# Expert layer of a two-block transformer: gate and up products with resting weights, free slots with an index past the last row

## Chip, cores and metric

One core of one Trainium2 chip runs one program. The metric is the device time of that program in microseconds (us), as a median over runs. TensorE (PE) has two clock levels, 1.2 and 2.4 GHz; the profile gives the granted clock as a share of the higher one.

## What is computed

512 tokens of 1024 features go through two transformer blocks. The first (latent attention, retention, convolution) and all of the second block but its last layer are not touched by the change. That last layer is a mixture of 16 experts; each token goes to 2 of them, both from one group of 4. `hf` below is the normalised token matrix (512 x 1024), `combine` holds for each token the weights of its two experts and zeros elsewhere, and the result is added to the residual.

```python
def _hier_moe(h, w_r1, b_r1, w_r2, b_r2, w_gate, w_up, w_down):
    ...
    g_sel = jnp.argmax(g_logits, axis=-1)
    ...
    top_p, top_i = lax.top_k(e_prob, EXPERT_TOPK)
    ...
    combine = jnp.sum(jax.nn.one_hot(expert_id, N_EXPERTS, dtype=jnp.float32)
                      * (g_w * top_p)[..., None], axis=1)
    hid = jax.nn.silu(jnp.einsum('nd,edf->nef', hf, w_gate)) * jnp.einsum('nd,edf->nef', hf, w_up)
    hid = hid * combine[..., None].astype(hid.dtype)
    out = jnp.einsum('nef,efd->nd', hid, w_down)
    return out.reshape(B, T, D)
```

Everything is float32. D_MODEL is 1024 and a hidden row of an expert has 256 features, so an expert has a gate and an up matrix of 1024 x 256 each and a down matrix of 256 x 1024.

## The kernel before

**Products of float32.** PE takes a fast form of float32 (float32r) that keeps fewer bits. A matrix that needs full accuracy is split into a high and a low float32r part (`split_w`, L337 on ACT rounds to the high part `wh`, L338 on DVE subtracts to the low part `wl`; both have a ring of three buffers), and `mm3` (L343 to L345) sums three products: high x high, low x high, high x low. A plain float32 matmul needs no split, and PE runs it as two passes, each with its own load of weights. "Weights" of a matmul, here, is the operand that rests in the PE array; the other moves through it.

**Experts.** An expert works on a block of NS = 96 slots. The experts' matrices come as 48 tiles of 1 MB (per expert: two tiles of gate and up side by side, four 128-row chunks of 512 columns each, then one of down), loaded by SP (`eraw`, `wraw` L1559) into NB = 14 buffers: N1 = 6, N0 = 2 and N2 = 3 buffers of their own and 3 of the general ring. A load past those waits for the load two before it; the thirteenth waits for the first gather.

**Routing** (`route`). For each of the four tiles of 128 tokens the block's last projection adds to the residual; `half` writes x times the norm's gain to a DRAM table `xgd` (Pool multiply L1608, store L1609) and x to the output (L1610), and forms the router's logits on PE (L1618). The norm's scale (`rsqrt`, L303 to L321) comes later and is not in `xgd`: it goes as two numbers per slot (`val`, L1713 to L1720) through a one-hot matmul (`look`, L1695) into `wsl`, and is applied in the tanh (L1790) and on the output (L1817, L1818). `slots` gives each slot the row it reads (L1745) and the row it adds to (L1748), which for a free slot is one of 96 spare rows behind the 512 of the output; these are written with x1 ahead of time (L1001).

**The loop.** For expert n: `gather` fetches 96 rows of `xgd` by an indirect DMA of Pool (L1763), PE transposes them (L1770, 8 times), ACT and DVE split them (L1772, L1773). `up`: the tokens rest (128 x 96) and the weights move (512 columns): 8 chunks x 3 matmuls into one PSUM bank of 96 x 512; then tanh L1790, L1791, L1792, two transposes back (L1795) and the split of the hidden rows (L1797 to L1800). For expert 0, Pool does the low part of three of the four splits (`n0`). `down`: hidden rows rest, two halves of 128 features; the second half is a plain float32 matmul (L1811) without a split, the first a split with 6 matmuls. Rows are weighted (L1817 on ACT, L1818 on DVE) and added to the output by an indirect DMA of Pool (L1819). In the program's loop, expert n's gather comes ahead of expert n-1's `up` and expert n-2's `down`; a scheduler sets the order on each engine. PSUM has four banks that `mm` hands out in turns.

Of the kernel before, what the change touches and what calls it, by code (L numbers as in the profile page):

```python
# [8 lines left out]
F32 = mybir.dt.float32  # L9
F32R = mybir.dt.float32r  # L10
# [10 lines left out]
RSK = 0.47077597149489786            # RSK * (t * t + RSB * t + RSC): t ** -0.5 within 3e-5 where RSQ brings t  # L21
# [103 lines left out]
class Cols:  # L125
    """Columns of a packed [128, n] array by name."""
# [18 lines left out]
def gain_cols(g):  # L145
    """Per-partition columns of the small vectors."""
# [25 lines left out]
def consts_a():  # L172
    """Tables of the first block: latent attention, retention."""
# [40 lines left out]
def consts_c():  # L214
# [10 lines left out]
    c.add("tok", np.stack([j, 512 + j], axis=1))  # L225
# [32 lines left out]
KT = [(48 + 128 * j, 128) for j in range(4)] + [(0, 48)]      # tiles of the compressed keys: tokens, the meta ones three times  # L258
# [4 lines left out]
class Kern:  # L263
# [14 lines left out]
    # ---- small helpers  # L278
# [18 lines left out]
    def rsqrt(s, ss, mult, name="rs", bufs=4):  # L297
        """(ss * mult + EPS) ** -0.5"""
# [16 lines left out]
        # y: the root with its sign turned; then a step of the third order and one of the second, both but for a factor  # L315
# [16 lines left out]
    def split_w(s, src, shape, eng=None):  # L332
        """src: [128, *shape] of 1024 elements -> (high, low) float32r parts"""
# [13 lines left out]
    def proj_f(s, raw, f, act, outs):  # L347
        """out[f-columns, tokens] for one 128-column half of a feature tile; outs: (psum, first token, tokens)"""
# [8 lines left out]
    def proj_all(s, raw, f, t0=0):  # L357
        """feature tile for the tokens from t0 on, the meta ones included: [(psum, their slice)]"""
# [9 lines left out]
    def proj_t(s, names, act, outs, by_tile=()):  # L368
        """out[tokens, 512 columns]; outs: (psum, first token, tokens); token tile by token tile in the halves by_tile"""
# [19 lines left out]
    def sumsq(s, src, n=128):  # L389
        """sums of squares of the rows of src"""  # L390
# [6 lines left out]
    def parts(s, p, sq):  # L397
        """sq in three exact bf16 parts; sq is spent"""
# [7 lines left out]
    def colsums(s, q, ps):  # L406
        """ps[token, tile]: sums over the rows of parts q"""
# [4 lines left out]
    def norm_T(s, src, n, gain, dst, off, ss=None):  # L412
        """rms-norm of n token rows, transposed into dst (high, low) at column off"""
# [17 lines left out]
    def split_y(s, y, k, scale=None):  # L431
        """y fp32 [128, 512] -> chunk k of yT"""
# [8 lines left out]
    # ---- block 1  # L441
# [56 lines left out]
    def silu2(s, p, z, tag, shape=None, bufs=2):  # L498
        """2 * silu(z)"""
# [8 lines left out]
    def rope_t(s, p, src, n, i, dst):  # L508
        """dst [n, 4, 64] = rope(src) by the token tables of tile i"""
# [58 lines left out]
            # states before each token tile, two heads on a diagonal  # L568
# [90 lines left out]
            # rotated shared keys, token-major  # L659
# [45 lines left out]
    def mla(s, lat, fill):  # L705
        nc, gc, id_ = s.nc, s.gc, s.id
        with s.pool("ml", 2) as p:
# [24 lines left out]
            def pull(n):  # L732
                """n more projections of convolution and gates"""
# [5 lines left out]
            def prep(g):  # L739
                """keys, values and queries of two heads"""  # L740
# [70 lines left out]
            def front(g):  # L811
                """scores and their exponentials, by query tiles"""
# [698 lines left out]
class Kern3(Kern2):  # L1511
    def moe(s):
        nc, a = s.nc, s.a
        with ExitStack() as c3:
# [12 lines left out]
            for n in range(N1 + N0, N1 + N0 + NF):  # L1527
                s.eraw(n)
# [373 lines left out]
```

## Time and profile before

| quantity | value |
|---|---|
| runs | 1320.57, 1323.01, 1323.64 us |
| median | 1323.01 us |
| span of the profiled execution, first to last instruction | 1319.7 us |
| PE busy | 1253.8 us, 95% of the span |
| DVE, ACT, POOL busy | 815.0, 585.1, 157.1 us |
| expert stage, first transposes to last matmul | 1136.8 to 1307.0 us |
| DMA share in most of that stage (1141 to 1240 us) | 1.01 |

The records do not say which of the three runs was profiled; the median is 3.3 us above the span. In the profile, a line such as L1763 is a line of the kernel, "out<-in" are the program's names of tiles, PEld is the load of weights, and a DMA share of 1.00 means that all 16 DMA engines of the core are busy throughout.

### The profile page before, as it was taken

What the parts mean: (1) busy time and instruction counts of PE and PEld (TensorE: products, weight loads), DVE (VectorE), ACT (ScalarE), POOL (GpSimd) and SP (SyncE); (2) the same over time, 40 slices, a digit from 0 to 9 for tenths busy, and PEclk for the clock granted to TensorE, in tenths of its full rate; (3) what the DMA queues carried; (4) which work ended last, traced back from release to release, by engine and by line L of the source; (5) the groups of instructions that cost most, each with busy time, mean ns of one, the idle gap of its engine ahead of it and who ended that gap; (6) DMA issues with size and microseconds to landing.
All of it is one profiled execution on the core that took longest, in us unless ns stands there. A gap on an engine that the chain in (4) does not pass through costs nothing. (4 is left out here: it accounts for less than half of the span.)

```text
span 1319.7 us, 17112 instructions
## 1 busy us (share of the span) xinstructions
PE 1253.8 (95%) x6356; PEld 982.0 (74%) x6356; DVE 815.0 (62%) x1869; ACT 585.1 (44%) x1053; POOL 157.1 (12%) x194
## 2 busy tenths in 40 slices
PE   6999999999999999999989999999999998799985
PEld 4788777877886787887777887888888887566652
DVE  6356776656866899325677534465563245898863
ACT  4233455444564453223556326333332243377762
POOL 0330110100000000000211111000002213223211
PEclk9999999999999999999999999999999999799997
DMA  7212121034541102222110131321245365699994
GB/s 260 98 65 80 49 73 41 25 106 170 210 159 66 52 34 76 96 96 72 58 64 33 65 125 36 116 76 61 100 150 192 109 236 182 195 320 314 313 287 120
DMA packets 31566, 164.12 MB, mean 124 GB/s; under 512 B 3746, under 2 KB 6690, under 8 KB 15588
## 3 DMA queue, kind: packets, MB, share of 16 engines
q1 hardware_dynamic: 27028, 147.65, 32.2%
q0 software_dynamic: 3584, 12.58, 4.4%
q10 hardware_dynamic: 864, 2.72, 0.6%
q8 instruction: 52, 0.85, 0.3%
q14 instruction: 38, 0.31, 0.1%
HBM read 150.36 MB, written 12.98 MB: 124 GB/s over the span
## 5 line engine op out<-in xcount | busy, mean ns | idle before, releaser
L338 DVE TENSOR_TENSOR wl<-raw,wh 128x1024 fp32r<-128x1024 f32 x167 | 213.5, 1279 | 177.2 <-ACT wh L337 166.5
L337 ACT ACTIVATE wh<-raw 128x1024 fp32r<-128x1024 f32 x167 | 176.4, 1059 | 312.5 <-PE mmp L344 216.5
L344 PE MATMUL mmp<-hl,wh 128*128 128x512 f32 (+1 forms) x488 | 192.6, 395 | 0.0
L343 PE MATMUL mmp<-hh,wh 128*128 128x512 f32 (+1 forms) x488 | 192.5, 395 | 0.0
L345 PE MATMUL mmp<-hh,wl 128*128 128x512 f32 (+1 forms) x488 | 192.1, 394 | 0.3 <-DVE wl L338 0.3
L345 PEld LDWEIGHTS mmp<-hh,wl 128*128 128x128 f32 x488 | 91.9, 188 | 19.7 <-issue 1.0
L343 PEld LDWEIGHTS mmp<-hh,wh 128*128 128x128 f32 x488 | 91.8, 188 | 19.3 <-issue 1.0
L344 PEld LDWEIGHTS mmp<-hl,wh 128*128 128x128 f32 x488 | 91.8, 188 | 18.6 <-issue 0.8
L338 DVE TENSOR_TENSOR wl<-eraw,wh 128x1024 fp32r<-128x1024 f32 x62 | 75.6, 1222 | 17.7 <-ACT wh L337 15.8
L337 ACT ACTIVATE wh<-eraw 128x1024 fp32r<-128x1024 f32 x65 | 68.7, 1057 | 25.7 <-PE mmp L345 15.4
L344 PE MATMUL mmp<-yl,wh 128*128 128x512 f32 x192 | 75.8, 396 | 0.0
L345 PE MATMUL mmp<-yh,wl 128*128 128x512 f32 x192 | 75.7, 395 | 0.0
L343 PE MATMUL mmp<-yh,wh 128*128 128x512 f32 x192 | 75.5, 396 | 0.0
L343 PE MATMUL mmp<-uh,wh 128*128 128x512 f32 (+3 forms) x160 | 55.6, 347 | 1.1 <-DVE cz L493 1.1
L344 PE MATMUL mmp<-ul,wh 128*128 128x512 f32 (+3 forms) x160 | 56.0, 351 | 0.0
L345 PE MATMUL mmp<-uh,wl 128*128 128x512 f32 (+3 forms) x160 | 55.2, 345 | 0.0
L343 PE MATMUL mmp<-wh,xh 128*96 128x512 f32 x128 | 52.3, 409 | 0.0
L343 PE MATMUL mmp<-wh,yh 128*128 128x512 f32 x128 | 50.6, 401 | 1.6 <-DVE xr L929 1.4
L345 PE MATMUL mmp<-wh,yl 128*128 128x512 f32 x128 | 51.9, 408 | 0.0
L344 PE MATMUL mmp<-wl,yh 128*128 128x512 f32 x128 | 51.7, 404 | 0.0
L344 PE MATMUL mmp<-wl,xh 128*96 128x512 f32 x128 | 51.4, 402 | 0.0
L345 PE MATMUL mmp<-wh,xl 128*96 128x512 f32 x128 | 50.6, 395 | 0.0
(546 smaller groups left out, 2751.4 us busy)
## 6 DMA issues: line engine op xcount, KB each, us to landing
raw<-in_wt_dram SPq DMA_DIRECT2D x85, 1024.0 KB, 5.0
eraw<-in_wt_dram SPq DMA_DIRECT2D x39, 1024.0 KB, 8.2
xin<-in_x_dram SPq DMA_DIRECT2D x4, 512.0 KB, 8.0
xr<-in_x_dram SPq DMA_DIRECT2D x4, 512.0 KB, 4.3
x<-xr SPq DMA_DIRECT2D x4, 512.0 KB, 4.5
rxr<-x SPq DMA_DIRECT2D x8, 256.0 KB, 3.1
out_dram<-rxr SPq DMA_DIRECT2D x8, 256.0 KB, 2.1
xgd<-rxg SPq DMA_DIRECT2D x8, 256.0 KB, 3.0
```

What stands on the lines that cost most here:

```text
L337: nc.scalar.activation(h, src, AF.Copy)
L338: (eng or nc.vector).tensor_tensor(l, src, h.bitcast(F32), op=ALU.subtract)
L343: mm(ps, ah, bh, start=start, stop=False)
L344: mm(ps, ah, bl, start=False, stop=False)
L345: mm(ps, al, bh, start=False, stop=stop)
```

## The change

1. **`up` with resting weights.** A 128 x 128 piece of the weights rests and the tokens move. The first tile of an expert is taken as it is: 16 plain float32 matmuls (4 chunks x 4 column groups) with 96 moving columns. The second is split as before: 16 pairs of a matmul of `wh` with the tokens' high and low parts side by side (192 columns) and one of `wl` with the high part (96). So two of the four splits of `up` go, and half of the tokens' features needs no split. The result is the hidden rows transposed, in two PSUM banks (gate, up); a copy and an add join the two parts of each (L1799, L1800), and the two transposes of the hidden rows go.
2. **`down` splits both halves** of its tile: one split more, and 12 float32r matmuls in place of 6 and 2 plain ones. `ye` has 2 buffers instead of 3.
3. **Normalised table.** ACT multiplies x times gain by the norm's scale before the store to `xgd` (two instructions per token tile, and the stores come that much later); `wsl` is one number per slot, `V` has 6 columns instead of 9.
4. **Free slots** get an index of 512 or more, and gather and scatter skip what is past row 511. The spare rows' x1 store and `dst` go. As a skipped row leaves its buffer as it was, `blank` clears the four `xg` buffers once, on Pool.
5. **N2 is 4**, so NB is 15. Pool splits nothing for expert 0.

```diff
@@ constants, route
-N1, N0, N2 = (6, 2, 3)
+N1, N0, N2 = (6, 2, 4)
...
-                    nc.sync.dma_start(a['out'][T:], s.x1[:NS])
...
-            xg = q.tile([128, 512], F32, tag='xg', name='rxg', bufs=3)
+            xg = q.tile([128, 512], F32, tag='xg', name='rxg', bufs=5)
...
-            ts(hr[:, i:i + 1], r, 0.5, None, op0=ALU.mult)
+            for z in range(2):
+                xg = xgs.pop((i, z))
+                nc.scalar.activation(xg, xg, AF.Copy, scale=r)
+                nc.sync.dma_start(s.xgd[128 * i:128 * i + 128, 512 * z:512 * z + 512], xg)
@@ slots
-        nc.vector.tensor_copy(a, tb[:, :, 0])
-        tt(idx, tb[:, :, 1], a, op=ALU.add)
-        nc.vector.tensor_scalar(u, tb[:, :, 2], -1.0, 1.0, op0=ALU.mult, op1=ALU.add)
-        tt(a, tb[:, :, 1], a, op=ALU.add)
-        nc.vector.scalar_tensor_tensor(dst, u, s.ce['tok'][:NS, 1:2], a, op0=ALU.mult, op1=ALU.add)
+        nc.vector.tensor_scalar(a, tb[:, :, 2], -float(T), float(T), op0=ALU.mult, op1=ALU.add)
+        tt(a, a, tb[:, :, 0], op=ALU.add)
+        tt(idx, a, tb[:, :, 1], op=ALU.add)
@@ blank, gather
+        for _ in range(2):
+            s.nc.gpsimd.memset(p.tile([128, D], F32, tag='xg', name='xg', bufs=2)[:NS], 0.0)
...
+                                         bounds_check=T - 1, oob_is_err=False)
...
+            if z:
+                nc.scalar.activation(xs[:, :, 0], b, AF.Copy)
+                nc.vector.tensor_tensor(xs[:, :, 1], b, xs[:, :, 0].bitcast(F32), op=ALU.subtract)
+            else:
+                nc.scalar.activation(xf, b, AF.Copy)
@@ up
+        ps = [s.mm()[:, :4 * NS].rearrange('p (f z c) -> p f z c', f=2, z=2) for _ in range(2)]
+        w = raws[0].rearrange('p (k c) -> p k c', k=4)
+        for k in range(4):
+            for f in range(4):
+                mm(ps[f // 2][:, f % 2, 0], w[:, k, 128 * f:128 * f + 128], xf[:, k], start=k + f % 2 == 0, stop=False, skip_group_check=True)
+        w = raws[1].rearrange('p (k c) -> p k c', k=4)
+        for j in range(2):
+            h, l = s.split_w(w[:, 2 * j:2 * j + 2], [2, 512])
+            for kk in range(2):
+                k = 2 * j + kk
+                for f in range(4):
+                    fc = slice(128 * f, 128 * f + 128)
+                    mm(ps[f // 2][:, f % 2], h[:, kk, fc], xs[:, k], start=False, stop=False, skip_group_check=True)
+                    mm(ps[f // 2][:, f % 2, 0], l[:, kk, fc], xs[:, k, 0], start=False, stop=k == 3, skip_group_check=True)
+        for z in range(2):
+            nc.scalar.activation(gu[z], ps[z][:, :, 1], AF.Copy)
+            nc.vector.tensor_tensor(gu[z], gu[z], ps[z][:, :, 0], op=ALU.add)
+        nc.scalar.activation(th, gu[0], AF.Tanh, scale=0.5)
...
@@ down
-        for c in range(2):
-            nc.tensor.matmul(po[c], hf, w[:, 1, 512 * c:512 * c + 512], start=True, stop=False)
-        h, l = s.split_w(w[:, 0], [1024])
+        for k in range(2):
+            h, l = s.split_w(w[:, k], [1024])
...
-        y = p.tile([128, D], F32, tag='ye', name='ye', bufs=3)[:NS]
+        y = p.tile([128, D], F32, tag='ye', name='ye', bufs=2)[:NS]
```

On PE, one expert in the middle of the loop before (mmp is a PSUM bank of `mm`, atp one for transposes, xh and xl the tokens' parts, hs the hidden rows' parts, eraw and raw tiles of weights; eight times the three rows with xh and xl, two of which are left out here):

```order
L1770 MATMUL atp<-id,xg 128x96 x8
L343 MATMUL mmp<-wh,xh 96x512
L344 MATMUL mmp<-wl,xh 96x512
L345 MATMUL mmp<-wh,xl 96x512
...
L1811 MATMUL mmp<-eraw,hf 96x512 x2
L343 MATMUL mmp<-wh,hs 96x512
L1795 MATMUL atp<-id,eth 128x96 x2
```

After L1795 there follow five more of the rows with hs. And one expert after the change:

```order
L1769 MATMUL atp<-id,xg 128x96 x8
L1787 MATMUL mmp<-xf,eraw 128x96 x16
L1795 MATMUL mmp<-xs,wh 128x192
L1796 MATMUL mmp<-xs,wl 128x96
...
L343 MATMUL mmp<-wh,hs 96x512
L344 MATMUL mmp<-wl,hs 96x512
L345 MATMUL mmp<-wh,hs 96x512
```

The pair L1795, L1796 stands 16 times, the three rows with hs 4 times. 24 moving passes of 512 columns became 64 loads of 128 columns with 96 or 192 moving ones, and nothing of the next expert stands between two `down` matmuls.

On DVE, one expert in the middle after the change, where the first row is the low part of `down`'s second piece and the two rows L1800 release the two PSUM banks of `up`:

```order
L338 TENSOR_TENSOR wl<-eraw,wh 128x1024
L1800 TENSOR_TENSOR gu<-gu,mmp 128x192
L1803 SCALAR_TENSOR_TENSOR eth<-eth,gu 128x192
L338 TENSOR_TENSOR wl<-raw,wh 128x1024
L1800 TENSOR_TENSOR gu<-gu,mmp 128x192
L338 TENSOR_TENSOR wl<-raw,wh 128x1024
L1804 TENSOR_TENSOR eth<-eth,gu 128x192
L1823 TENSOR_SCALAR ye<-mmp,wsl 96x512
L1807 TENSOR_TENSOR hs<-eth,hs 128x192
```

The release of the second bank stands behind a split of the next expert's weights; ACT has the same pattern (wh, gu, eth, wh, gu, wh). Four splits per expert stand where there were five.

On Pool, ahead of the first gather, before:

```order
L1608 TENSOR_TENSOR rxg<-rxr,gff 128x512 x4
L338 TENSOR_TENSOR wl<-eraw,wh 128x1024
L1608 TENSOR_TENSOR rxg<-rxr,gff 128x512 x3
L338 TENSOR_TENSOR wl<-eraw,wh 128x1024 x2
L1608 TENSOR_TENSOR rxg<-rxr,gff 128x512
L1763 DMA xg<-xgd,idx 96x1024 x8
```

and now:

```order
L1754 MEMSET xg 96x1024 x2
L1608 TENSOR_TENSOR rxg<-rxr,gff 128x512 x8
L1754 MEMSET xg 96x1024 x2
L1761 DMA xg<-xgd,idx 96x1024 x8
```

The three splits went to DVE, and two memsets stand right ahead of the first gather; the second of them waits for the last stores of rxg to `xgd`, whose memory it takes over.

## Rows read from the trace of the kernel before

**Rows 1.** The page: busy time (share of the span) and instructions by engine.
```profile
PE 1253.8 (95%) x6356; PEld 982.0 (74%) x6356; DVE 815.0 (62%) x1869; ACT 585.1 (44%) x1053; POOL 157.1 (12%) x194
```
**Rows 2.** Windows: stretch, us, busy (instructions) by engine, PEclk, DMA share, GB/s.
```profile
1141.40:1240.00 98.60, 98.60 (x456) 64.48 (x454) 87.93 (x114) 76.88 (x113) 26.09 (x20) 1.00 1.01 312
1240.00:1297.00 57.00, 49.82 (x210) 32.02 (x209) 40.37 (x51) 33.73 (x51) 7.91 (x5) 0.94 0.91 292
```
**Rows 3.** DMA queues in 1136.8 to 1297 us: packets, MB, share of 16 engines.
```profile
q1 hardware_dynamic: 5184, 37.75, 66.8%
q0 software_dynamic: 3102, 10.87, 30.3%
```
**Rows 4.** Timeline of PE over one expert: start, duration, line, operation, tiles.
```profile
1174.92 0.82 PE L1770 MATMUL atp<-id,xg 96*128 96x96 f32 x8
...
1176.28 0.40 PE L343 MATMUL mmp<-wh,xh 128*96 128x512 f32 x1
...
1180.90 0.39 PE L345 MATMUL mmp<-wh,xl 128*96 128x512 f32 x1
...
1184.49 0.83 PE L1770 MATMUL atp<-id,xg 96*128 96x96 f32 x8
1185.10 0.45 PE L343 MATMUL mmp<-wh,xh 128*96 128x512 f32 x1
```
**Rows 5.** Timeline of PE, three places with short matmuls.
```profile
1106.31 0.99 PE L1618 MATMUL mmp<-wr,h2T 128*128 128x24 f32 x8
1107.14 0.47 PE L345 MATMUL mmp<-wh,yl 128*128 128x512 f32 x1
...
623.98 0.27 PE L343 MATMUL atp<-dkh,dq 128*128 128x128 f32 x1
...
624.20 0.40 PE L343 MATMUL atp<-dkh,dq 128*128 128x384 f32 x1
...
155.64 0.28 PE L345 MATMUL mmp<-uh,wl 128*128 128x258 f32 x1
...
157.07 0.28 PE L345 MATMUL mmp<-uh,wl 128*128 128x258 f32 x1
```
**Rows 6.** PEld by line: count, duration ns min/median/max, first and last start, forms.
```profile
L1770 PEld LDWEIGHTS atp<-id,xg x128: 137/141/231, 1136.8 to 1277.7; 96*128 96x128 f32 x128
L1618 PEld LDWEIGHTS mmp<-wr,h2T x64: 186/192/333, 1078.2 to 1125.5; 128*128 128x128 f32 x64
```
**Rows 7.** Groups by form, 1140 to 1300 us: busy, mean ns, idle before, releasers.
```profile
L338 DVE TENSOR_TENSOR wl<-eraw,wh 128x1024 fp32r<-128x1024 f32 x62 | 75.6, 1222 | 17.7 <-ACT wh L337 15.8
L337 ACT ACTIVATE wh<-eraw 128x1024 fp32r<-128x1024 f32 x62 | 65.5, 1057 | 21.1 <-PE mmp L345 10.8 <-DMA eraw<-in_wt_dram 7.4 <-SPq L1542 2.3
L1792 DVE TENSOR_TENSOR eth<-eth,mmp 96x256 f32<-96x256 f32 x16 | 6.7, 417 | 0.6
```
**Rows 8.** Timelines of DVE, POOL and PE at the start; last a group of POOL.
```profile
1121.44 2.26 DVE L321 SCALAR_TENSOR_TENSOR rs<-rsu,rsy 128x1 f32<-128x1 f32 x1
...
1126.48 0.16 DVE L321 SCALAR_TENSOR_TENSOR rs<-rsu,rsy 128x1 f32<-128x1 f32 x1
...
1121.34 2.35 POOL L338 TENSOR_TENSOR wl<-eraw,wh 128x1024 fp32r<-128x1024 f32 x1 [3.80 <-ACT wh L337]
...
1132.26 1.12 POOL L1763 DMA_INDIRECT xg<-xgd,idx  x1 [7.36 <-DVE val L1715]
...
1136.79 1.54 PE L1770 MATMUL atp<-id,xg 96*128 96x96 f32 x8 [1.00 <-DMA xg<-xgd,idx]
...
L1082 POOL MEMSET wa2f<- 96x512 f32 x1 | 0.5, 523 | 94.5 <-DMA raw<-in_wt_dram 94.5
```
**Rows 9.** The tail: last matmul of PE, a piece of the chain, last scatter.
```profile
1306.62 0.40 PE L345 MATMUL mmp<-wh,hs 128*96 128x512 f32 x1
...
1303.37 5.37 DMA out_dram<-ye,dst
...
1309.59 1.41 POOL L1819 DMA_INDIRECT out_dram<-ye,dst  x1 [4.81 <-DMA out_dram<-ye,dst]
```

More of the change, by code (lines that the diff above doesn't have):

```diff
@@ L224, in consts_c @@
     c.add("iota", np.tile(j[:NS], (128, 1)))
-    c.add("tok", np.stack([j, 512 + j], axis=1))
+    c.add("tok", j)
     c.add("nblk", np.tile(np.arange(NX), (128, 1)))
@@ L1598, in route @@
         oh = one("oh", 4, 2, NS, dt=BF)
-        r4, hr = one("r4", 4), one("hr", 4)
+        r4 = one("r4", 4)
         s.wk = q
@@ L1605, in half @@
             ss = s.sumsq(xv)
[L1606 removed]
+            xg = q.tile([128, 512], F32, tag="xg", name="rxg", bufs=5)
             rc = (slice(128 * i, 128 * i + 128), slice(512 * c, 512 * c + 512))
             nc.gpsimd.tensor_tensor(xg, xv, g[:, rc[1]], op=ALU.mult)
[L1609 removed]
+            xgs[i, c] = xg
             nc.sync.dma_start(s.a["out"][rc], xv)
@@ L1624, in get @@
             return xr
-        part = {}
+        part, xgs = {}, {}
         def done(i, c, xv, b):
@@ L1687, in route @@
         s.out_t("wp", get, done)
-        s.idx, s.dst, s.wsl = one("idx", 16, dt=I32), one("dst", 16, dt=I32), one("wsl", 16, 2)
-        tb = one("tb", 16, 6)
+        s.idx, s.wsl = one("idx", 16, dt=I32), one("wsl", 16)
+        tb = one("tb", 16, 3)
         def look(z0, z1):
@@ L1696, in look @@
             return pi
-        s.slots(look(0, 3), 16, s.idx, s.dst)
+        s.slots(look(0, 3), 16, s.idx)
         ge, sg, w, sw = one("ge", 4, 4), one("sg", 4), one("w", 4, 2), one("sw", 4)
@@ L1709, in route @@
         tt(w, w, sw[:, :, None].to_broadcast([128, 4, 2]), op=ALU.mult)
[L1711 to L1722 removed]
+        ts(w, w, 0.5, None, op0=ALU.mult)
+        for z in range(3):
+            cp(V[:, :, :, 3 + z], w)
+            if z < 2:
+                tt(w, w, V[:, :, :, 3 + z], op=ALU.subtract)
+        fill(0, 4, 3, 6)
+        cp(tb[:NS], look(3, 6))
         s.weights(tb, s.wsl)
@@ L1753, in weights, with blank @@
         tb, wsl = tb[:NS], wsl[:NS]
-        t3 = tb.rearrange("p e (v z) -> p e v z", z=3)
-        tt(wsl, t3[:, :, :, 0], t3[:, :, :, 1], op=ALU.add)
-        tt(wsl, wsl, t3[:, :, :, 2], op=ALU.add)
+        tt(wsl, tb[:, :, 0], tb[:, :, 1], op=ALU.add)
+        tt(wsl, wsl, tb[:, :, 2], op=ALU.add)
+    def blank(s, p):
+        for _ in range(2):
+            s.nc.gpsimd.memset(p.tile([128, D], F32, tag="xg", name="xg", bufs=2)[:NS], 0.0)
     def gather(s, idx, p=None):
@@ L1816, in down @@
-        y = p.tile([128, D], F32, tag="ye", name="ye", bufs=3)[:NS]
-        nc.scalar.activation(y[:, :512], po[0], AF.Copy, scale=wsl[:NS, 1:2])
-        nc.vector.tensor_scalar(y[:, 512:], po[1], wsl[:NS, 1:2], None, op0=ALU.mult)
+        for k in range(2):
+            h, l = s.split_w(w[:, k], [1024])
+            for c in range(2):
+                cs = slice(512 * c, 512 * c + 512)
+                s.mm3(po[c], hh[:, k], hl[:, k], h[:, cs], l[:, cs], k == 0, k == 1)
+        y = p.tile([128, D], F32, tag="ye", name="ye", bufs=2)[:NS]
@@ L1819, in down @@
+        nc.scalar.activation(y[:, :512], po[0], AF.Copy, scale=wsl[:NS])
+        nc.vector.tensor_scalar(y[:, 512:], po[1], wsl[:NS], None, op0=ALU.mult)
         nc.gpsimd.indirect_dma_start(out=s.a["out"], out_offset=bass.IndirectOffsetOnAxis(ap=dst[:NS], axis=0), in_=y, in_offset=None,
-                                     compute_op=ALU.add)
+                                     compute_op=ALU.add, bounds_check=T - 1, oob_is_err=False)
     def overflow(s, p):
@@ L1866, in overflow @@
                         nc.vector.tensor_scalar(oh, s.iota, rk[:, i, k:k + 1], None, op0=ALU.is_equal)
-                        nc.tensor.matmul(pi[:NS, :9], oh, s.V[:, i, k], start=i + k == 0, stop=i + k == 4)
-                idx, dst = (q.tile([128, 1], I32, tag=f"oi{z}", name="oi", bufs=2) for z in range(2))
-                wsl = q.tile([128, 1, 2], F32, tag="ow", name="ow", bufs=2)
-                tb = q.tile([128, 1, 9], F32, tag="otb", name="otb", bufs=2)
-                nc.vector.tensor_copy(tb[:NS], pi[:NS, :9].rearrange("p (e z) -> p e z", z=9))
-                s.slots(tb, 1, idx, dst)
+                        nc.tensor.matmul(pi[:NS, :6], oh, s.V[:, i, k], start=i + k == 0, stop=i + k == 4)
+                idx = q.tile([128, 1], I32, tag="oi", name="oi", bufs=2)
+                wsl = q.tile([128, 1], F32, tag="ow", name="ow", bufs=2)
+                tb = q.tile([128, 1, 6], F32, tag="otb", name="otb", bufs=2)
+                nc.vector.tensor_copy(tb[:NS], pi[:NS, :6].rearrange("p (e z) -> p e z", z=6))
+                s.slots(tb, 1, idx)
                 s.weights(tb[:, :, 3:], wsl)
-                hid = s.up(p, s.gather(idx), raws[:2], wsl[:, 0])
-                s.down(p, hid, raws[2], wsl[:, 0], dst)
+                hid = s.up(p, s.gather(idx), raws[:2])
+                s.down(p, hid, raws[2], wsl, idx)
 def body(nc, tc, a):
```

86 lines of the change are left out of this document (28 added, 58 removed).

## Prediction, made before the changed kernel ran

> **What bounds the kernel now.** I read the page's shares first: PE is busy 95% of a span of 1319.7 us, and no other engine comes near [rows 1]. A share over the whole span says little about one stage, so the windows come next: from 1141.4 to 1240 us PE has no idle time at all at full clock, and the DMA engines stand at 1.01; from 1240 to 1297 PE is idle 57.0 - 49.8 = 7.2 us and its clock falls to 0.94, with the DMAs at 0.91 [rows 2]. The expert stage thus has two parts: in the first, PE works off tiles that were loaded ahead and sets the pace; in the second that stock is used up, and the weight loads set it. The DMA queues say what the loads share the engines with: weights (q1) take 66.8% of the window and the indirect gathers and scatters (q0) 30.3% [rows 3].
>
> The timeline of PE gives the period of the first part: two starts of the transposes lie 1184.49 - 1174.92 = 9.57 us apart [rows 4]. Between 1176.28 and 1180.90 lie 20 steps of 512-column matmuls, so one costs 4.62 / 20 = 0.231 us; the eight transposes hold PE for 1185.10 - 1184.49 = 0.61 us, 77 ns each [rows 4]. Sixteen periods from the first transposes at 1136.79 [rows 8], and some 3 us for the slow start, would end at 1293; the last matmul really ends at 1307.0 [rows 9]. The 14 us between are the price of the second part: idle time and matmuls at the lower clock behind loads.
>
> **The change, part by part.**
>
> *PE per expert.* The changed period is 64 passes of a 128-column load with 96 or 192 moving columns (16 plain float32 matmuls of two passes, 32 float32r), 12 matmuls of 512 columns, 8 transposes. The price of a pass is the main choice. From below: the transposes' 77 ns, which are a load of 128 columns and a short move too [rows 4]. Then eight float32 passes with 24 moving columns, 1107.14 - 1106.31 = 0.83, or 0.104 each; two float32r matmuls of 128 columns, 624.20 - 623.98 = 0.22, or 0.110 each; from above, 258 moving columns: 12 steps in 157.07 - 155.64 = 1.43, or 0.119 each [rows 5]. I take 0.110, the row with the same load, number type and nearly the same columns. The load records back this: 192 ns for a float32 load of 128 columns against 141 ns in the transposes [rows 6], a difference of 51 ns that is more than the whole distance from 0.077 to 0.110. So 64 x 0.110 = 7.04, 12 x 0.231 = 2.77, transposes 0.61, changeovers 0.05: 10.47 us. PE streams fewer columns than before and yet takes longer, since each short move waits for the next load.
>
> *Waits in the period.* The last pass of `up` is followed on PE by 2.77 of `down`, 0.61 of transposes and the first four passes of the next `up` (0.44), 3.82 us in all, and then the next `up` writes the second PSUM bank. Its release runs: copy on ACT, add on DVE, tanh on ACT, then `wh` on ACT (1.06) and `wl` on DVE (1.22) of the next expert, which stand ahead of the second add. No row has the new small operations; the nearest, a DVE operation of 96x256 from PSUM, took 0.417 [rows 7]. Four of them at 0.35 (192 columns) to 0.42 give 1.4 to 1.7; with 2.28 for the split and some 0.2 of hand-overs the loop is 3.9 to 4.2 us. I take a stall of 0.13, so the period is 10.6 us; the ends are 0 and 0.4. ACT and DVE themselves have room: four splits of 1.06 and 1.22 are 4.2 and 4.9 us, and the rest some 3 us each, of 10.6.
>
> *DMA.* 1024 of the 1536 slots hold a token (two for each of 512), so skipping the others would take a third of q0's time: 0.303 x 160.2 / 3 = 16 us of all engines in this stage [rows 3]. One tile more is loaded ahead of the stage. At a period of 10.6 a weight tile is wanted every 3.53 us where before it was every 3.19. Loads needed 0.668 x 160.2 = 107 us and the rest of q0 32 us, so they would end some 140 us after the start, near 1277 to 1283, and PE would need the last tile only at about 1300. PE is then never behind loads, and the 14 us of the second part go. This holds even if skipped slots cost as much traffic as before: the loads would then end near 1296.
>
> *Start.* Before, a DVE operation of one column took 2.26 us where the same line takes 0.16 later, exactly while a split ran on Pool [rows 8]; two such stalls lie on the way to the first gather, 4.2 us together. They go, but DVE gets two splits of 1.22 there (2.4 us). A memset of 96 x 1024 is about twice that of 96 x 512 (0.523) [rows 8], some 1.0 us, and one of two waits for the last store to `xgd`, which now comes after the scale and two more ACT operations; I take 0.3 us net for the part that the index doesn't hide. Net: 1.5 us earlier, first transposes at 1135.3. The ends are 4 earlier and 1.5 later.
>
> *End.* Scatters are ordered: the last one waited for the one before it, whose landing took 5.37 us, and the program ended 10.1 us after the last scatter began [rows 9]. After the change, ACT and DVE order puts the split of expert 15's hidden rows behind the output rows of expert 14, so `down` of 15 starts about 1.1 us after `down` of 14 and ends 3.9 after it. The scatter of 14 starts about 1.5 us after `down` 14, lands 5.4 later, and the last starts 0.85 after that: 1.5 + 5.4 + 0.85 + 10.1 = 17.9 after `down` 14, or 14.0 after the last matmul. Before it was 1319.7 - 1307.0 = 12.7.
>
> *Edits at nothing.* Three fewer columns of `V`, no `dst`, no x1 store, the ACT scale of the first three token tiles: all beside the last projection, whose PE work goes on. Two buffers of `ye` for three: a buffer is wanted 10.6 us after its predecessor, and a scatter lands in far less than twice that.
>
> **The sum.** 1135.3 + 16 x 10.6 (169.6) + 3.0 for the start (transposes at the lower clock took 1.54 us where they take 0.82 later [rows 4, 8], the wait for the first copies, the first matmuls at that clock) + 1.1 at the end gives 1309.0 for the last matmul, against 1307.0. With 14.0 behind it the span is 1323.0, 3.3 us more than before. The median of the three runs, 1323.01, is 3.3 above the profiled span; I keep that offset: **1326.3 us, call it 1326**. In short: 16.5 us more in the periods, 14 less behind loads, 1.5 less at the start, 1.3 more at the end, and a remainder of rounding. About 0.3%, or 4 us, is what a measurement of this kernel can tell from no change.
>
> **Rivals.**
>
> *Passes at the transposes' pace (faster).* If 77 ns held for the resting weights, the period on PE would be 64 x 0.077 + 2.77 + 0.61 + 0.05 = 8.4 us, loads would become the bound throughout, and end near 1278. Before, the last tile landed at about 1297, where the window of [rows 2] ends, and the program ended 23 us later; the same gives a span near 1301 and a time near 1304. Against it: the float32 and float32r rows [rows 5, 6]; for it, nothing but that the transposes are so fast. The Trainium skill (TensorE: Matmul & The Clock Gate, section Back-to-back issue gap) states about 81 ns as the measured spacing of a load and a matmul of 128 columns in a stream of such pairs. By that rule the passes would take 64 x 0.081 = 5.2 us and the period would be 8.6, this rival's case; the trace disagrees for float32r, with 0.110 us at the same 128 columns. Chance 0.11.
>
> *Passes at the lower price and no stall (a little faster).* At 0.104 the passes take 6.66, the period is 10.1 and the time 16 x 0.5 = 8 us lower, 1318. A start 4 us earlier would add to it. Chance 0.15.
>
> *The bank's release decides (slower).* Place: the second add behind the split of the next expert on DVE and ACT. Price: each 0.1 us in the loop beyond 3.82 costs 1.6 us in all; the point from which it decides is a loop of about 4.2. At 4.3 the stall is 0.5, the period 11.0 and the time 1332; with passes at 0.119 besides, the period is 11.5 and the time up to 1340. For it: nothing on PE stands between `up`s but `down`. Against it: the sums above end near 4.0. Chance 0.20.
>
> *The skip saves no traffic.* The change then does less than it says, and the time is the same as forecast, as PE is ahead of the loads in neither case. I count it in the forecast.
>
> *The clock falls* as PE waits on loads of weights more of the time. In the stage now the granted clock is 1.00 where PE is busy throughout [rows 2], and nothing in the changed stage leaves PE idle. At half the clock each period would be about twice as long, 160 us in all. Chance 0.03.
>
> **How the numbers follow.** The forecast's own case (period 10.4 to 10.8) has 0.51 and gives 1322 to 1330. Faster by over 0.3% is below 1319.0: the first rival and most of the second, 0.22. Slower by over 0.3% is above 1327.0: the bank, the clock and a third of the forecast's case, 0.40; between them 0.38. The range of 1313 to 1337 leaves out the first rival, the clock and the worst of the bank.
>
> **What would show it.** The gathers' spacing is the period: 10.5 to 10.7 bears me out, 8.4 to 9 is the first rival, 11 or more the bank, and then L1787 waits on DVE's L1800. Weight loads end before 1285 with gaps; q0's share falls by a third; the first gather starts near 1130.5; DVE has no 2 us operation of one column; the last scatter waits for the one before it. I am wrong at the root if PE waits for weight tiles late in the stage.

## The result, and the profile after

The changed kernel takes 1331.68 us (median of six runs, 1328.16 to 1336.41) against 1323.33 for the kernel before in the same comparison: a ratio of 1.0069, with a 95% interval of 1.0042 to 1.0096. The forecast was 1326 with a range of 1313 to 1337. The time lies in the range, but on the slower side of the 0.3% that can be told apart, which had a chance of 0.40. The six runs lie in two groups of three, 1328.2 to 1328.9 (mean granted clock 0.987 to 0.988) and 1334.5 to 1336.4 (0.980 to 0.982). The profile shown here is of the lower group, 1328.16; every run's time is 1.8 us above its own span. The experiments come back to the two groups.

PE is still the busiest engine. Busy time and share on the page of the changed kernel, against [rows 1]:

```profile
span 1326.4 us, 18408 instructions
PE 1266.9 (96%) x6996; PEld 1037.1 (78%) x6996; DVE 792.6 (60%) x1864; ACT 575.1 (43%) x1061; POOL 161.9 (12%) x195
```

The windows of the changed kernel, with the columns of [rows 2] (stretch, us, busy and instructions by engine, PEclk, DMA share, GB/s):

```profile
1136.00:1140.00 4.00, 4.00 (x22) 3.77 (x20) 0.56 (x1) 1.59 (x4) 1.15 (x2) 0.50 0.91 267
1140.00:1280.00 140.00, 140.00 (x1115) 129.56 (x1115) 92.20 (x141) 80.93 (x141) 36.84 (x23) 0.99 0.95 309
1280.00:1303.00 23.00, 22.48 (x178) 20.64 (x177) 14.18 (x22) 13.21 (x21) 4.33 (x3) 1.00 0.21 33
```

The second part of the stage, in which PE waited for loads before [rows 2], is gone: PE is busy for 140.0 of 140.0 us, and the DMA share falls to 0.21 from 1280 on, since the last load ends before 1282. PEld, the load of weights, is busy for 129.6 of those 140 us where it was 64.5 of 98.6 before. The DMA queues of the changed kernel between 1136 and 1297 us, against [rows 3]:

```profile
q1 hardware_dynamic: 5184, 37.75, 67.1%
q0 software_dynamic: 2923, 6.97, 19.8%
```

The weights are the same, and the gathers and scatters took a third less of the engines' time. What went is bytes: over the whole program q0 moves 8.40 MB instead of 12.58, in the same 3584 packets, so a skipped row still has a packet, a small one. The timeline of PE over one expert of the changed kernel, against [rows 4]:

```profile
1189.05 0.82 PE L1769 MATMUL atp<-id,xg 96*128 96x96 f32 x8
1189.71 3.80 PE L1787 MATMUL mmp<-xf,eraw 128*128 128x96 f32 x32
1193.30 0.34 PE L1795 MATMUL mmp<-xs,wh 128*128 128x192 f32 x1
...
1196.89 0.43 PE L343 MATMUL mmp<-wh,hs 128*96 128x512 f32 x1
...
1199.70 0.82 PE L1769 MATMUL atp<-id,xg 96*128 96x96 f32 x8
```

From start to start: transposes 0.66, the 32 plain float32 passes 3.59 (0.112 each), the 32 float32r passes 3.59 (0.112 each), `down` 2.81, together 10.65 us where it was 9.57. A float32r pass of 192 columns and one of 96 cost the same on average as a float32 pass of 96. The matmuls of PE wait only twice between 1140 and 1310 us:

```profile
PE mmp L343 <- ACT hs L1806: 2.7, 1, 2.7
PE mmp L1787 <- DVE gu L1800: 0.5, 1, 0.5
```

So the PSUM banks' release, which L1787 waits for, decides only once, and PE never waits for a load. The 2.7 us are in the tail. There the timelines of PE, DVE and POOL of the changed kernel read, against [rows 9]:

```profile
1305.97 0.40 PE L345 MATMUL mmp<-wh,hs 128*96 128x512 f32 x1
1309.10 0.74 PE L343 MATMUL mmp<-wh,hs 128*96 128x512 f32 x1 [2.73 <-ACT hs L1806]
...
1305.76 1.22 DVE L338 TENSOR_TENSOR wl<-eraw,wh 128x1024 fp32r<-128x1024 f32 x1 [0.59 <-ACT wh L337]
1306.90 0.35 DVE L1800 TENSOR_TENSOR gu<-gu,mmp 128x192 f32<-128x192 f32 x1
1307.16 1.22 DVE L338 TENSOR_TENSOR wl<-eraw,wh 128x1024 fp32r<-128x1024 f32 x1
...
1308.57 0.74 DVE L1823 TENSOR_SCALAR ye<-mmp,wsl 96x512 f32<-96x512 f32 x1
...
1310.08 1.41 POOL L1824 DMA_INDIRECT out_dram<-ye,idx  x1 [8.73 <-DVE hs L1807]
1316.32 1.41 POOL L1824 DMA_INDIRECT out_dram<-ye,idx  x1 [4.83 <-DMA out_dram<-ye,idx]
```

`down` of expert 14 ends at about 1306.2. From 1305.76 on DVE does two splits for `down` of 15, an add and a multiplication (L1804) before it comes to the output rows of 14 (L1823 at 1308.57), so the scatter of 14 starts 3.9 us after that end; the hidden rows of 15 come later still, and PE waits 2.7 us and goes on at half clock (0.50 between 1309 and 1312 us, with 0.43 us from a matmul to the next, 0.23 later).

### The profile page after: what moved, and what is told of

Same layout as the page of the kernel before. It is cut to its first block, busy times and chain, and to the rows that moved or that the text cites. A ratio compares the mean times of both kernels' runs of the same rounds, so it can differ in the third digit from the quotient of the medians.

```text
span 1326.4 us, 18408 instructions
## 1 busy us (share of the span) xinstructions
PE 1266.9 (96%) x6996; PEld 1037.1 (78%) x6996; DVE 792.6 (60%) x1864; ACT 575.1 (43%) x1061; POOL 161.9 (12%) x195
## 3 DMA queue, kind: packets, MB, share of 16 engines
q0 software_dynamic: 3584, 8.40, 3.0%
HBM read 149.97 MB, written 12.58 MB: 123 GB/s over the span
## 4 chain that ended last, share of the span: by engine, by line
PE 74%; issue 10%; DVE 8%; ACT 4%; DMA 2%; POOL 1%; SPq 0%; POOLq 0%; DVEq 0%; ACTq 0%
PE mmp L343 16%; PE mmp L345 16%; PE mmp L344 16%; PE mmp L1787 4%; PE mmp L1795 3%; DVE wl L338 1%; PE mmp L1796 1%; PE atp L825 1%; PE obp L868 1%; ACT sm L1342 1%; ACT wh L337 1%; PE obp L343 1%; PE atp L1769 1%; PE atp L343 1%; PE obp L345 1%
## 5 line engine op out<-in xcount | busy, mean ns | idle before, releaser
L338 DVE TENSOR_TENSOR wl<-raw,wh 128x1024 fp32r<-128x1024 f32 x164 | 209.8, 1280 | 183.1 <-ACT wh L337 173.1
L337 ACT ACTIVATE wh<-raw 128x1024 fp32r<-128x1024 f32 x164 | 173.1, 1058 | 318.6 <-PE mmp L344 217.4
L338 DVE TENSOR_TENSOR wl<-eraw,wh 128x1024 fp32r<-128x1024 f32 x52 | 63.5, 1220 | 45.8 <-ACT wh L337 45.2
L337 ACT ACTIVATE wh<-eraw 128x1024 fp32r<-128x1024 f32 x52 | 54.5, 1049 | 44.3 <-PE mmp L1796 30.6
L1795 PE MATMUL mmp<-xs,wh 128*128 128x192 f32 x256 | 59.0, 321 | 0.0
L1796 PE MATMUL mmp<-xs,wl 128*128 128x96 f32 x256 | 57.3, 229 | 0.0
L1787 PE MATMUL mmp<-xf,eraw 128*128 128x96 f32 x416 | 51.4, 283 | 0.5 <-DVE gu L1800 0.5
```

Of the source, the lines that this page charges most:

```text
L337: nc.scalar.activation(h, src, AF.Copy)
L338: (eng or nc.vector).tensor_tensor(l, src, h.bitcast(F32), op=ALU.subtract)
L1787: mm(ps[f // 2][:, f % 2, 0], w[:, k, 128 * f:128 * f + 128], xf[:, k], start=k + f % 2 == 0, stop=False, skip_group_check=True)
L1795: mm(ps[f // 2][:, f % 2], h[:, kk, fc], xs[:, k], start=False, stop=False, skip_group_check=True)
L1796: mm(ps[f // 2][:, f % 2, 0], l[:, kk, fc], xs[:, k, 0], start=False, stop=k == 3, skip_group_check=True)
```

## The experiments

**Theories.** A: the resting weights lengthen PE's period, because each pass costs its load, and the skipped slots take the DMA engines' load away; the two pull in opposite directions. B: the loads lag behind for a reason of their own, and the skip does little. C: the two groups of runs are a matter of PE's clock at one place (C2 and C3, below, say where and what would mend it). D: a pass (one load and one move) costs its load whatever moves. E: the tail is lengthened by the order on DVE.

**The skip alone.** The kernel before, with:

```diff
-                    st[n] = [s.gather(s.idx[:, n:n + 1], p if n % 4 > 1 else None)]
+                    st[n] = [s.gather(s.dst[:, n:n + 1], p if n % 4 > 1 else None)]
...
+                                         bounds_check=T - 1, oob_is_err=False)
...
+            s.blank(s.xgp)
...
+            s.blank(p)
```

> The kernel before with one part of the change alone: gather and scatter take the index that lies past row 511 for a free slot and skip it, and the gather buffers are cleared once. Theory A (in the kernel before, the second part of the expert stage, 14 us, is the price of loads that share the DMA engines with gathers and scatters; PE itself needs 9.57 us per expert): the period stays 9.57 us to the end, no idle PE after 1240 us, last matmul about 1137 + 1 + 153 + 3 = 1294, span about 1306, time 1307 to 1310. Theory B (those 14 us are the loads' own chain, each waiting for the one two before it, whatever else the DMA engines do): time 1320 or more, PE idle after 1240 as before.

Measured: 1315.87 us (12 runs), a ratio to the kernel before of 0.9956 (0.9937 to 0.9976). The windows of its profile (1312.94 us):

```profile
1142.00:1260.00 118.00, 118.00 (x546) 76.88 (x545) 106.20 (x137) 91.83 (x137) 28.49 (x21) 1.00 0.95 302
1260.00:1285.00 25.00, 23.10 (x106) 15.02 (x105) 20.02 (x25) 16.95 (x26) 3.19 (x2) 1.00 0.89 300
1285.00:1297.00 12.00, 8.86 (x31) 4.36 (x29) 4.64 (x8) 4.23 (x7) 2.82 (x2) 1.00 0.27 57
```

PE's first pause comes at 1268.3 us instead of 1250.2, and the clock stays up after 1260. So the loads do suffer from the gathers and scatters, as theory A has it, but neither theory's number came: the gain is 0.44% where A expected about 1% and B none. PE still waits 4.6 us in its last experts, three times for DVE's L1799, and ahead of each of them a split of weights had waited on ACT: twice for a load (2.8 us), and twice for what the profile gives as SyncE (3.4 us), while the last loads were landing. So the last loads are still late. Whether that is the DMA engines, whose share is 0.89 up to 1285 us, or the order of the loads, each of which waits for the one two before it, these runs do not show.

**Without the resting weights.** The change, with `gather`, `up` and `down` of the kernel before (and skipped slots in them):

```diff
-        xf, xs = x
...
+        xh, xl = x
+        ps = s.mm()[:NS]
...
+        nc.scalar.activation(th, ps[:, :256], AF.Tanh, scale=0.5)
...
+        nc.scalar.activation(y[:, :512], po[0], AF.Copy, scale=wsl[:NS])
...
-            xg = q.tile([128, 512], F32, tag="xg", name="rxg", bufs=5)
+            xg = q.tile([128, 512], F32, tag="xg", name="rxg", bufs=4)
```

> The change with its resting weights undone: gather, up and down as before (moving weights, five splits per expert), everything else of the change kept (normalised table, skipped free slots, 15 buffers, no splits on Pool; the scaled halves have 4 buffers instead of 5). Theory A: first transposes at 1134.8 as after the change, period 9.57, last matmul about 1291, span about 1304, time 1305 to 1308. Theory B: the loads fall behind again, time 1318 or more. If the resting weights themselves save something that the trace of the change does not show, this kernel is slower than 1331.

Measured: 1310.82 us (six runs, 1308.5 to 1315.6), ratio 0.9921 (0.9896 to 0.9946). That is 3 us above what theory A expected and 7 below B's number. It is the fastest kernel of the study and beats both the kernel before and the change: all of the change but its first two parts is worth 0.8%, and the first two parts, the resting weights and the `down` that goes with them, take back about 1.5%. The gathers show the period; from the first to the last of these nine are eight periods:

```profile
1157.58 1.43 POOL L1761 DMA_INDIRECT xg<-xgd,idx  x1 [0.30 <-issue]
...
1234.67 1.64 POOL L1761 DMA_INDIRECT xg<-xgd,idx  x1 [0.30 <-PE mmp L345]
```

77.09 / 8 = 9.64 us. Against the change that is 1.01 less, 16 us for 16 experts; the profiled spans differ by 17.6 (1308.8 and 1326.4). The six runs of this kernel have clocks of 0.987 or 0.988: it has no upper group.

**The resting weights with the old traffic.** The change, with:

```diff
-        nc.vector.tensor_scalar(a, tb[:, :, 2], -float(T), float(T), op0=ALU.mult, op1=ALU.add)
...
+        tt(idx, tb[:, :, 1], a, op=ALU.add)
...
+        nc.vector.scalar_tensor_tensor(dst, u, s.ce["tok"][:NS, 1:2], a, op0=ALU.mult, op1=ALU.add)
...
-                                         bounds_check=T - 1, oob_is_err=False)
...
+                    nc.sync.dma_start(a["out"][T:], s.x1[:NS])
```

> The change without the skip: free slots read row 0 and add to a spare row of their own, as before; all else of the change kept. Theory A: PE's period of 10.65 leaves the loads ahead even so; they end some 12 us later than the 1283 of the change, near 1296, and the time is that of the change within 3 us. Theory B: loads are late in the last experts, PE waits for them, and the time is 5 us or more above that of the change.

Measured: 1327.79 us (seven runs), ratio 1.0051 (1.0024 to 1.0078), beside 1327.97 and 1.0069 (1.0043 to 1.0095) for the change in the same comparison. The window at the end shows the loads and the spare traffic running on, a DMA share of 0.50 where the change has 0.21, and PE just as busy:

```profile
1280.00:1300.00 20.00, 19.49 (x152) 17.76 (x150) 13.09 (x21) 11.53 (x19) 3.33 (x2) 1.00 0.50 114
```

The time is the one that theory A expected; the loads end near 1288, earlier than its 1296. So skipping the free slots, worth 0.44% to the kernel before, is worth nothing that can be measured beside the resting weights: PE is then the slower of the two in either case.

**Half the moving columns.**

```diff
-mm(ps[f // 2][:, f % 2, 0], w[...], xf[:, k], ...)
+mm(ps[f // 2][:, f % 2, 0, :48], w[...], xf[:, k, :48], ...)
-mm(ps[f // 2][:, f % 2], h[:, kk, fc], xs[:, k], ...)
+mm(ps[f // 2][:, f % 2, 1], h[:, kk, fc], xs[:, k, 1], ...)
```

> The change with fewer moving columns in up and as many loads: the plain float32 matmuls move 48 tokens instead of 96, the wh ones move 96 columns (the low parts alone) instead of 192. It leaves out half of the first tile's tokens and the high x high product. Theory D (a resting-weight pass costs its load, 0.11 us, whatever moves): the period between gathers stays at 10.65 us within 0.1, time within 3 us of the change. Rival (the moving columns or something per column set the pace): the columns fall from 7680 to 4608 per expert, so 64 passes fall by up to 40%, 2.8 us, period 8 to 9.5, time below 1310.

Measured: 1383.77 us (four runs), ratio 1.0489 (1.0456 to 1.0521), mean clock 0.943. Neither theory foresaw this time. A piece of PE's timeline at full clock and two windows of its profile:

```profile
1198.12 3.70 PE L1787 MATMUL mmp<-xf,eraw 128*128 128x48 f32 x32
1201.64 0.29 PE L1795 MATMUL mmp<-xs,wh 128*128 128x96 f32 x1
```
```profile
1198.00:1203.00 5.00, 5.00 (x47) 5.00 (x46) 3.65 (x6) 1.92 (x4) 2.40 (x2) 0.97 0.64 228
1203.00:1212.00 9.00, 9.00 (x34) 7.50 (x34) 3.80 (x6) 4.31 (x7) 0.00 (x0) 0.50 0.88 284
```

At full clock 32 passes of 48 columns take 3.52 us, 0.110 each, against 0.112 with 96: half the columns save 2%, so the columns do not set the pace. That alone could also be a fixed price per pass. Rows of the kernel before, with the clock at 1.00 in both places, settle it:

```profile
142.94 0.97 PE L799 MATMUL mmp<-ones,sq 96*128 96x1 f32 x8
143.78 0.48 PE L345 MATMUL mmp<-uh,wl 128*128 128x512 f32 x1
...
180.20 0.22 PE L868 MATMUL obp<-PTh,Vl 128*64 128x128 f32 x1
...
180.80 0.22 PE L868 MATMUL obp<-PTl,Vh 128*64 128x128 f32 x1
```

Eight passes with a load of 128 columns and one moving column take 0.84 us, 0.105 each; ten steps of passes that load 64 columns and move 128 take 0.60, 0.060 each. The price follows the columns that are loaded, so theory D's price stands. Its time does not: in the middle of the passes, at about 1202.7, the granted clock falls to its lower level and stays there through the other passes and the twelve matmuls of `down`, with PE busy for 9.00 of 9.00 us. The mean clock is 0.67 to 0.82 in every 20 us from 1180 to 1360, and that is what costs the 55 us.

**The upper group.** The change once more:

> The changed kernel once more, as its six runs lie in two groups, 1328.2 to 1328.9 and 1334.5 to 1336.4 us, with mean granted clocks of 0.987 to 0.988 and 0.980 to 0.982. Theory C (a stretch of some 13 us falls to half clock in some runs and costs about half of that): the two groups come again, 6 to 7 us apart, and a profile of the slower group shows one more stretch at 0.5. Rival (the groups are an accident of those runs): one group.

Nine runs: five at 1324.4 to 1328.0 (clock 0.986 to 0.988), four at 1333.8 to 1336.2 (0.980 to 0.981). The groups are there again, and the profile fell in the lower one. One run more:

> The changed kernel once more, for a profile. If it falls in the group near 1334 (about four of ten do): by theory C2 a stretch of 15 to 17 us at half clock that the profile of the lower group has not, in the passes of the first two experts, before the first down; passes there 0.22 us instead of 0.11. If in the lower group: nothing new.

It fell in the upper group, 1333.18 us at 0.981. Its windows, and three rows of PE's timeline in the first of them:

```profile
1134.00:1152.00 18.00, 18.00 (x90) 18.00 (x90) 4.81 (x8) 4.98 (x10) 3.40 (x3) 0.50 0.94 308
1152.00:1280.00 128.00, 128.00 (x1005) 117.70 (x1004) 84.22 (x130) 75.16 (x130) 35.53 (x21) 0.99 0.93 303
```
```profile
1141.87 0.51 PE L1795 MATMUL mmp<-xs,wh 128*128 128x192 f32 x1
1142.17 0.34 PE L1796 MATMUL mmp<-xs,wl 128*128 128x96 f32 x1
1142.31 0.49 PE L1795 MATMUL mmp<-xs,wh 128*128 128x192 f32 x1
```

In this run PE is at half clock for all of 1134 to 1152 us, through the first expert's passes and into the second's, and a pair costs 0.44 us instead of 0.22. Half clock ends at 1153.8 here and at 1141.4 in the profile of the lower group, each time in the middle of resting passes. The 12.4 us more at half clock (some 13 were expected at first, then 15 to 17) lose 6.2 us, about the distance between the groups (medians 1328.55 and 1335.0 of the first six runs). PE is busy throughout here too. Theory C holds, and the place is the stage's start.

**Work ahead of the first passes.** The change, and the kernel without resting weights, with matmuls that serve nothing while PE waits for the first rows (the comments stand here only):

```diff
+        wb = s.mm()[:NS]
+        def warm(n, src):
+            for j in range(n):
+                nc.tensor.matmul(wb, oh[:, 3, 1], src[:, 256:768], start=True, stop=True)
+        warm(4, ...)     # after the slots' lookup
...
+        warm(5, ...)     # after the weights' lookup; 18 in the last of the three kernels
```

> The change with nine matmuls of 512 columns that serve nothing, put where PE waits before the first transposes (four after the slots' lookup, five after the weights' lookup). Theory C2 (in the runs of the change near 1334 the first experts' resting-weight passes stay at half clock; PE comes to them from idle, and whether the clock rises there is decided run by run): with PE at work on 512 columns just before, no run lies in the upper group (none above 1331, no mean clock under 0.984), the first 4 us at half clock shrink to under 1, and the rest lie 1 to 3 us below the lower group of the change (1324 to 1328). Rival (the upper group's stretch at half clock lies elsewhere, or the groups are no matter of the clock): about four of ten runs still near 1333.

> The change without resting weights, with the same nine matmuls ahead of the first transposes. Before its start costs some 4 us at half clock: the median falls by 1 to 3 us from the 1310.8 of no_rest. Rival (the half clock at the start is hidden behind loads): the same within 1 us.

> As change_warm, but 22 of the idle matmuls, 18 of them from the weights' lookup on: 512 columns without a gap for some 5 to 7 us, which holds up the first transposes by some 3 us. Theory C3 (the clock rises on matmuls of 512 columns, and the resting passes that follow then hold it): the clock is 1.00 before the first resting pass, no run above 1331, median 1325 to 1329, all clocks 0.986 or more. Rival (resting passes at the stage's start do not hold or raise the clock, whatever ran before): at least four of ten runs above 1331 as before, and a profile of such a run with half clock in the first experts.

With nine, the change took 1335.75 us (ratio 1.009, 1.0054 to 1.0125): five of six runs in the upper group, against what I expected. Its profile, of an upper run, has the clock at 0.50 from the idle matmuls through the first expert and into the second:

```profile
1126.00:1132.00 6.00, 5.75 (x25) 2.97 (x25) 4.81 (x34) 0.00 (x0) 3.38 (x4) 0.50 0.25 60
1132.00:1156.00 24.00, 23.96 (x118) 23.73 (x118) 6.15 (x14) 6.01 (x12) 4.40 (x4) 0.50 0.91 299
```

The nine ended before the clock had risen, and theory C2's remedy with nine of them is refuted. Without resting weights the nine changed nothing: 1312.75, ratio 0.9926 (0.9902 to 0.9950) beside 0.9921. With 22, all twelve runs of the change lie between 1324.78 and 1328.00, with clocks of 0.987 to 0.990: 1326.27, ratio 1.0040 (1.0023 to 1.0057). Windows of its profile and the timeline of PE there:

```profile
1130.00:1136.00 6.00, 6.00 (x30) 3.62 (x30) 3.14 (x21) 0.00 (x0) 3.33 (x4) 0.68 0.54 148
1136.00:1142.00 6.00, 6.00 (x58) 5.73 (x56) 1.12 (x2) 1.64 (x4) 1.91 (x2) 1.00 0.98 345
```
```profile
1131.87 4.60 PE L1706 MATMUL mmp<-R,oh 128*96 128x512 bf16 x16
1136.31 1.62 PE L1777 MATMUL atp<-id,xg 96*128 96x96 f32 x16
1137.77 3.74 PE L1795 MATMUL mmp<-xf,eraw 128*128 128x96 f32 x32
```

The clock is up before the first transposes (all 16 in 1.62 us where eight took 1.54), the first expert's 32 passes take 3.5 us, and the clock stays at 1.00 through the resting passes of the whole stage. Once up, the change's passes hold it; coming from the lower level, they sometimes leave it there. The counts of runs say less than this profile: of the twelve runs of the next experiment, on the same chip and with no idle matmuls, only two lie in the upper group, so none of twelve could be chance. The median with 22 is that of the change's lower group, no better.

**The tail.** The change, with the last expert's splits put behind other work (the comments stand here only):

```diff
+        if last:                   # down of expert 15
+            s.behind(a, s.gc1)     # wh of its splits after the second PSUM copy of up
+            s.behind(b, s.yd)      # wl after the output rows of expert 14
```

> The change with the order of its last expert mended: the high parts of down's splits for expert 15 are put behind the second PSUM copy on ACT, their low parts behind the output rows of expert 14 on DVE. Theory E (in the change these splits hold up the output rows of 14 by 2.4 us and the hidden rows of 15 by some 2 us): scatter of 14 starts about 2 us after the last matmul of down 14 instead of 3.9, down of 15 starts about 2 us after it instead of 2.9, and the span ends 2 us earlier, time 2 us below the change in runs of the same mean clock. Rival (the tail is set by the scatter alone): no difference beyond 0.5 us.

Measured: 1325.09 us (12 runs), ratio 1.0041 (1.0022 to 1.0061); the ten runs of the lower group lie at 1323.3 to 1326.8. The timelines of DVE and POOL, against those of the change above:

```profile
1305.52 0.74 DVE L1829 TENSOR_SCALAR ye<-mmp,wsl 96x512 f32<-96x512 f32 x1
...
1307.03 1.77 POOL L1830 DMA_INDIRECT out_dram<-ye,idx  x1 [6.82 <-ACT ye L1828]
1313.32 1.41 POOL L1830 DMA_INDIRECT out_dram<-ye,idx  x1 [4.51 <-DMA out_dram<-ye,idx]
```

`down` of 14 ends at 1305.1 there, so the scatter of 14 starts 1.9 us after it instead of 3.9, and the last scatter begins 8.2 us after it instead of 10.1. Theory E holds with its 2 us in the profile: the span ends 17.9 us after `down` of 14 instead of 20.2. One step came otherwise: `down` of 15 starts 0.2 us after that of 14 and waits 1.6 us for a split in its middle. The times agree, the median of the lower group being 1.9 us below that of the lower group in the change's nine runs, but these are runs of two chips, and by the ratios the difference is not clear of noise.

**One buffer less.** The kernel without resting weights, with N2 = 3:

> The change without resting weights, with 14 buffers instead of 15 (N2 = 3). If the tile held ahead matters once loads and PE are nearly in step (PE 9.6 us per expert against some 9.1 of loads), loads fall behind near the end: PE idle after 1240 us grows by up to 3 us and the time by 2 to 3 us over the 1310.8 of no_rest. If loads are well ahead until the last tiles: the same time within 1 us.

Measured: 1315.61 us (12 runs, 1309.41 to 1319.67), ratio 0.9960 (0.9941 to 0.9980), against 0.9921 (0.9896 to 0.9946) with 15 buffers. The medians differ by more than expected, 4.8 us, but the runs spread over 10 us and the intervals overlap; its one profile, of the fastest run, has no more idle PE than no_rest. That the tile held ahead is worth something without the resting weights is likely; how much stays open. With 0.9960 this kernel, which has the skip, the normalised table and no splits on Pool, lies where the skip alone lies (0.9956). So next to the skip, the table and Pool's free hands have shown no gain of their own.

## Why the prediction was right or wrong

The time of 1331.68 lies 5.4 us above the 1326.3 forecast. Three terms make that up: the span of the profiled run is 3.4 longer than forecast, the offset was put 1.5 too high, and the median lies 3.5 above the profiled run. The period and the loads were right; the end was mis-sized, and the clock was wrong in its mechanism.

*The period* (10.6): right at 10.65, in part by luck. The pass was taken at 0.110 and costs 0.112, `down` at 2.77 and costs 2.81, transposes and changeovers at 0.66 and cost 0.66: 10.65 without a stall, where the forecast had 10.47 and a stall of 0.13. That stall does not exist; the missing 0.18 happened to be nearly as large. The rival of a deciding release is refuted by the waits: 0.5 us in all. The rival of passes at the transposes' 77 ns is refuted by the timeline's 0.112. The reason given, that a short move waits for the next load, is borne out by the passes that load 64 columns and take 0.060. The Trainium skill (TensorE: Matmul & The Clock Gate, section Back-to-back issue gap) gives about 81 ns for a load and a matmul of 128 columns in a stream. The trace disagrees with it for float32 and float32r, with 0.112.

*The loads*: right. They end before 1282 (forecast 1277 to 1283), PE never waits for them, and the skip makes no difference beside resting weights, as the experiment with the old traffic shows.

*The start* (first transposes at 1135.3): right in the profile, 1134.75; over the later profiles of the change it lay between 1132.3 and 1134.8. DVE's stall of 2 us is gone, as forecast: its longest operation of one column on the way takes 1.23.

*The end* (17.9 us behind `down` 14, or 14.0 behind a last matmul that comes 3.9 after it): the term that was mis-sized. I saw in the order that hidden rows of 15 come behind the output rows of 14, but not that the output rows themselves stand behind two splits, an add and a multiplication. The scatter of 14 started 3.9 us after `down` 14 instead of 1.5, and the last matmul came 6.9 after it. The end of `down` 14 was forecast at 1305.1 and came at 1306.2; the span's end came 20.2 us after it. Together 3.4 us, the span's whole miss (1326.4 for 1323.0).

*The offset*: 3.3 us were added to the span because the median stood 3.3 above it. Each run's time is 1.8 above its own span; the profiled execution of the kernel before was simply 1.5 below the median. This made up part of the tail's miss, by luck.

*The clock*: the step that failed. I wrote that nothing in the changed stage leaves PE idle, gave a falling clock 0.03, and read the 1.00 of [rows 2] as what a busy PE gets. The runs show that PE can be busy without a pause and still be at the lower level: for 18 us at the stage's start in the upper group, which has 8 of the 16 runs of the change and costs 6 to 7 us each. With three of six runs in it, the median lies 3.5 us above the profiled run; with four of nine, in the second comparison, it is 1327.97. That the clock stayed up through the rest of the stage was luck as far as the forecast goes: its reason, that PE is not idle, did not keep the clock up with half the columns. Busy is the profile's word here, and it models the ends of matmuls. Why the clock stays low in some runs and not in others stays open. The Trainium skill (TensorE: Matmul & The Clock Gate, section HAM oscillation) names gaps of idle PE as what brings the clock down. The half-columns kernel disagrees, with the clock at 0.50 over 9.00 us of which PE is busy 9.00.

*The size of the balance*: I put the gain from the second part and the start at 15.5 us and the loss in the periods at 16.5. Without resting weights the kernel gains 0.8%, some 10 us, in part since PE still waits 2.1 us late in the stage and the period is 9.64 instead of 9.57; the periods lost 16 x 1.08 = 17.3.

## What to carry to other kernels

A matmul with resting weights and few moving columns is priced by its load: here 0.112 us per 128 columns of float32 weights, whether 48, 96 or 192 columns move, so fewer streamed columns are no gain unless there are fewer columns to load; here half the columns cost 55 us by the clock. A change of several parts can hide a good one: here the parts beside the headline are worth 0.8%, and the headline costs more than that; undo the headline first. An average over a window can hide when an engine was full: a DMA share of 0.69 was 0.89 while loads ran and 0.27 after them. A time with two groups of runs asks for a look at the granted clock of both before anything else is made of the median.

## What the runs showed of the hardware

- PE's granted clock fell from 1.00 to 0.50 in the middle of passes that load 128 columns and move 48 or 96 (half_columns), and stayed there over 9.00 us with PE busy for all of it. With 96 and 192 columns it stayed up for the rest of the stage once up (0.99 as a mean from 1140 to 1280), and stayed at 0.50 for 18 us in a run where the stage began there (change_look).
- Nine idle matmuls of 512 columns before the stage left the clock at 0.50 in the profile, and five of six runs lay in the upper group; 22 of them, 18 in a row but for four short matmuls, had it at 1.00 before the first pass in the profile, and no run of twelve lay in the upper group.
- A float32r pass and a plain float32 one with a load of 128 columns cost the same, 0.112 us at full clock and about 0.22 at half; a pass with a load of 64 columns and 128 moving ones cost 0.060.
- Skipped rows cost next to no transfer time: the queue of gathers and scatters fell from 30.3% to 19.8% of the engines' time in the stage, a third, as a third of the slots is free. The packets of the whole program stayed at 3584, with 8.40 MB instead of 12.58.
